# Where the third block's output projection stands, and which buffers wait for which

## The chip, the cores and the metric

The kernel runs on one core of one Trainium2 chip. The core has a matrix engine (TensorE, PE in the profile), VectorE (DVE), ScalarE (ACT), GpSimd (POOL) and SyncE (SP), which in this kernel issues all the data transfers in one queue. The metric is the device time of one execution in microseconds. Three runs of the kernel before took 2527.12, 2529.54 and 2530.48 us; the median is 2529.54 us.

## The reference

One decoder layer on 2112 tokens, 2048 of a prompt and 64 of eight running sequences, in f32. An input projection feeds two mixers, whose 512 + 512 rows are concatenated; an output projection, a norm and a SwiGLU feed-forward layer follow.

```
y5, h_re, h_im = s5_mixer(u, ...)          # ends in a GLU
yh, S_hg = hgrn2_mixer(q, fz, iv, og, ...) # 4 heads of 128
x = x + concatenate([y5, yh]) @ w_out      # 1024 x 1024
h2 = rmsnorm(x, norm_ffn)
x = x + (silu(h2 @ w_gate) * (h2 @ w_up)) @ w_down   # 2816 wide
y = rmsnorm(x, norm_final)
```

## The kernel before

Activations are stored feature by feature: 128 features on the partitions, tokens along the row. The mixers work through four groups of tokens and four heads, 16 heads in all. Beside the last heads, the generator `sides` (line 1332) runs the S5 mixer and its GLU, which writes its rows into the DRAM tensor `y_s`; each HGRN2 head writes its 128 rows there too.

What follows runs over three blocks of `FT = 704` tokens and has three kinds of product: the output projection (`mix`, matmul outputs named `o`), gate and up (`g`, `u`) and down (`d`). Each is done by a 2 x 2 block scheme with seven products in place of eight (`seven`, line 1073). Seven combinations of the activations, called slots here, meet seven combinations of the weights. Four of the seven slots are differences of the four quarters, made by `combine` (line 975). Every operand is split into a high and a low part (`xh`, `xl` for the activations, `wh`, `wl` for the weights), and a product is three matmuls of 128 x 352. One slot with two weight matrices is 24 matmuls.

- `combine_y` (line 988) makes the slots of block b for the projection: for each of four feature tiles it loads two row blocks of `y_s` (tile `cy`), makes four differences into `ct`, and stores them in DRAM as `ty_s`. For block 0 it runs in a pool `cmb` of two buffers, so that one tile follows the other; for blocks 1 and 2 it runs in the staging pool `xraw` (tiles `xr`).
- `x_slots` (line 1006) loads a slot into a staging tile `xr`, and ACT and DVE split it into `xh` and `xl`, for which there are 7 buffers, later 8. The staging pool has 1 buffer until block 0's projection is under way and 2 afterwards.
- `w_prep` (line 1020) loads two weight matrices at a time, makes their combinations in block 0 only, and splits them into `wh` and `wl`.
- `mix` adds the products on accumulators `acc`, eight tiles of 128 x 704 loaded from `xT`, and stores them in `x1_s`. `norm2` (line 1203) sums the squares (`sum_f`), brings the sum over the partitions with two pairs of small matmuls (`ss_f`, then `pr_f`), scales the eight accumulators in place (line 1207), makes the difference slots `ht` and stores all seven in `h_s`.
- `ffn` (line 1227) loads the slots of `h_s`, runs gate and up over 11 column pairs in three chunks `CH` of 4, 4 and 3, whose results become slots in `s_s`, and then down. The tiles `s`, `u` and `T` of gate and up come from the pool `hp2`.

The order before is: heads, `combine_y(0)`, `mix(0)`, `combine_y(1)` and `combine_y(2)`, `mix(1)` with `norm2(0)` after its first seven steps, `mix(2)` with `norm2(1)` likewise, `norm2(2)`, then `ffn` for the three blocks, each with the final norm of the block before inside it. A pool that is opened where another was closed takes over its memory, and its tiles wait for the last users of that memory (`reuse_waits`). `acc2` (4 accumulators) and the `ht` pool `mt` are closed before `hp2` is opened. A scheduling layer then orders the instructions on each engine; on the chip each engine works through its own list in order.

Of the kernel before, what the change touches and what calls it, by code (L numbers as in the profile page):

```python
# [9 lines left out]
F32 = mybir.dt.float32  # L10
# [8 lines left out]
P = 128  # L19
# [906 lines left out]
def glu(e, pool, ps, w):  # L926
    nc = e.nc
    wh, wl = w
    NB_ = 44
    W = NB_ * L  # L930
    for n0 in range(0, NCK, NB_):
        g = pool.tile([P, 4, L, NB_], F32, tag="gg", name=f"gg{n0}")
        for k in range(4):
            nc.sync.dma_start(g[:, k], e.g_s[k * P:(k + 1) * P, :, n0:n0 + NB_])
        hi = pool.tile([P, 4, L, NB_], F32R, tag="ghi", name=f"ghi{n0}")
        lo = pool.tile([P, 4, L, NB_], F32R, tag="glo", name=f"glo{n0}")
        nc.scalar.activation(hi, g, AF.Copy)
# [62 lines left out]
def y_slots(e, b):  # L1000
# [201 lines left out]
def norm2(e, b, x):  # L1202
    nc = e.nc
    r = norm_r(e, x, f"f{b}")
    for j in range(4):
        for d in (j, j + 4):
            nc.vector.scalar_tensor_tensor(x[d], x[d], e.gain[:, KD + d:KD + d + 1], r, op0=ALU.mult, op1=ALU.mult)
        B = [x[d][:, h * FH:h * FH + FH] for d in (j, j + 4) for h in range(2)]
        T = e.mtmp.tile([P, 4, FH], F32, tag="mt", name=f"ht{b}_{j}")
        combine(nc.vector, [T[:, i] for i in range(4)], *B)  # L1210
        dst = e.h_s[b]
        for slot, t in ((0, B[0]), (1, B[2]), (4, B[3])):
            nc.sync.dma_start(dst[:, slot, j], t)
        nc.sync.dma_start(dst[:, 2:4, j], T[:, 0:2])
        nc.sync.dma_start(dst[:, 5:7, j], T[:, 2:4])
# [8 lines left out]
            nc.sync.dma_start(e.o["yT"][d * P:(d + 1) * P, b * FT:(b + 1) * FT], x[d])  # L1224


def ffn(e, b, got):
    X = x_slots(e, [e.h_s[b][:, i] for i in range(7)], 4, f"h{b}")
    for c, (f0, nk) in enumerate(CH):
        for j in range(nk):  # L1230
            f = (f0 + j, f0 + nk + j)
            s = {}
            nm = f"{f[0]}_{b}"
            W = w_prep(e, [([e.i[w][i] for i in f], f"{n}{f[0]}") for w, n in (("w_gate_u", "g"), ("w_up_u", "u"))], 4, b)
            mats = [(W[0], gate_sink(e, s, nm), "g" + nm), (W[1], up_sink(e, s, nm, e.s_s[b][c], j), "u" + nm)]
            for _ in seven(e, mats, X, 4):
                yield
    x = acc_tiles(e, b, e.x1_s, f"d{b}")
    got["x"] = x
    for c, (f0, nk) in enumerate(CH):  # L1240
        X = x_slots(e, [e.s_s[b][c][:, i, :nk] for i in range(7)], nk, f"s{b}_{c}")
        cs = slice(f0 * P, (f0 + 2 * nk) * P)
        for g in range(2):
            js = (2 * g, 2 * g + 1)
            W = w_prep(e, [([e.i["w_down_u"][d][:, cs] for d in (j, j + 4)], f"wd{j}_{c}") for j in js], nk, b)
            mats = [(w, acc_sink(e, x[j], x[j + 4]), f"d{j}_{b}_{c}") for w, j in zip(W, js)]
            for _ in seven(e, mats, X, nk):
                yield


def run(gen, n=None):
    r = None
    i = 0
    while n is None or i < n:
        try:
            r = next(gen)
        except StopIteration:
            return r, True
        i += 1
    return r, False  # L1260
# [3 lines left out]
def body(ctx, tc, ins, outs, scratch=None, stop=9):  # L1264
    e = Env()
# [149 lines left out]
    for b in range(FB):
        ff = ffn(e, b, got[b])
        run(ff, 14)
        if b:
            final(e, b - 1, got[b - 1]["x"])
        run(ff)  # L1420
# [58 lines left out]
```

## Time and profile before

| what | value |
|---|---|
| median of three runs | 2529.54 us |
| profiled execution, its span | 2525.47 us, 2523.7 us |
| PE busy | 2313.9 us, 92% |
| DVE, ACT, POOL busy | 67%, 40%, 16% |
| mean granted TensorE clock | 0.958 |

The program has three parts. Until 829 us the mixers run, with PE busy throughout; from there to some 1174 us the projections and the first norms, with PE often idle; then gate, up and down until 2500 us. The last 24 us are the final norm of the last block. Busy shares of the whole say little here, since the middle part has limits of its own.

### The profile page before, as it was taken

The numbers are of one execution on the slowest core, as the hardware profiler recorded it, in microseconds if no ns is written. First come the engines' busy times: TensorE is split into PE (matmuls) and PEld (weight loads), VectorE is DVE, ScalarE is ACT, GpSimd is POOL, SyncE is SP. The second block draws the span as 40 slices with busy tenths as digits, with TensorE's granted clock in tenths as the row PEclk, the third lists the DMA queues.
The fourth block names the chain that finished last, engine by engine and source line by source line (L and its number), as shares of the span: only waits on it lengthen the run. The fifth ranks groups of instructions, "written<-read, shape, count | busy, mean of one in ns | idle before, by whom it ended". The sixth has DMA issues, their size and how long they took to land.

```text
span 2523.7 us, 44154 instructions
## 1 busy us (share of the span) xinstructions
PE 2313.9 (92%) x16933; PEld 2162.1 (86%) x16933; DVE 1700.1 (67%) x3222; ACT 1013.0 (40%) x1860; POOL 416.4 (16%) x807
## 2 busy tenths in 40 slices
PE   6999999999998463975999999999999999999997
PEld 5888777777787463965999999999999999999996
DVE  7936354555556575986777799865557786565776
ACT  4332323232222231642444544644455454444452
POOL 5209593948211000000000000000000000000000
PEclk9999999999999786987999999999999999999998
DMA  9696556444545679875665566676457567644752
GB/s 268 178 273 222 159 189 182 141 137 135 171 144 167 218 270 311 313 283 199 225 221 207 224 253 240 221 278 225 173 197 267 200 225 261 242 177 166 274 209 90
DMA packets 269317, 538.53 MB, mean 213 GB/s; under 512 B 82089, under 2 KB 172530, under 8 KB 256050
## 3 DMA queue, kind: packets, MB, share of 16 engines
q1 hardware_dynamic: 269106, 535.71, 61.9%
q8 instruction: 133, 2.18, 0.3%
q14 instruction: 78, 0.64, 0.1%
HBM read 373.06 MB, written 162.56 MB: 212 GB/s over the span
## 4 chain that ended last, share of the span: by engine, by line
PE 70%; DMA 10%; DVE 9%; POOL 7%; issue 2%; ACT 2%; SPq 1%; DVEq 0%; ACTq 0%; POOLq 0%
PE pA_u L1091 10%; PE pA_g L1091 10%; PE pA_d L1091 8%; PE pB_u L1091 5%; PE pB_g L1091 5%; PE pB_d L1091 4%; PE ps_v L263 3%; PE ps_u L263 3%; PE pQ_g L1091 3%; PE pQ_u L1091 2%; PE pQ_d L1091 2%; PE ps_f L263 2%; PE pz L263 2%; DMA cy<-y_s 2%; PE ps_q L263 2%
## 5 line engine op out<-in xcount | busy, mean ns | idle before, releaser
L1047 DVE TENSOR_TENSOR wl_g<-wr_g,wh_g 128x512 fp32r<-128x512 f32 x231 | 158.6, 687 | 114.2 <-ACT wh_g L1046 112.6
L290 POOL TENSOR_TENSOR r_z<-st_z,mhalf 128x2 f32<-128x2 f32 (+1 forms) x12 | 9.0, 765 | 1355.4 <-DVE st_z L289 1355.4
L1047 DVE TENSOR_TENSOR wl_u<-wr_u,wh_u 128x512 fp32r<-128x512 f32 x231 | 158.7, 688 | 98.5 <-ACT wh_u L1046 97.6
L1046 ACT ACTIVATE wh_g<-wr_g 128x512 fp32r<-128x512 f32 x231 | 144.6, 628 | 167.6 <-PE pA_g L1091 70.2
L1046 ACT ACTIVATE wh_wd<-wr_wd 128x512 fp32r<-128x512 f32 (+1 forms) x252 | 140.3, 589 | 176.1 <-DMA wr_wd<-in_w_down_u 81.2
L1046 ACT ACTIVATE wh_u<-wr_u 128x512 fp32r<-128x512 f32 x231 | 144.3, 628 | 151.3 <-DMA wr_u<-in_w_up_u 39.5
L1091 PE MATMUL pA_g<-xh_h,wh_g 128*128 128x352 f32 x528 | 172.9, 328 | 30.7 <-ACT s L1118 22.9
L1091 PE MATMUL pA_g<-xh_h,wl_g 128*128 128x352 f32 x528 | 172.6, 327 | 6.0 <-DVE wl_g L1047 6.0
L1091 PE MATMUL pA_g<-xl_h,wh_g 128*128 128x352 f32 x528 | 171.3, 324 | 0.0
L1091 PE MATMUL pA_d<-xh_s,wh_wd 128*128 128x352 f32 x528 | 170.3, 323 | 0.4 <-DVE acc_d L1106 0.4
L1091 PE MATMUL pA_u<-xh_h,wh_u 128*128 128x352 f32 x528 | 170.5, 323 | 0.0
L1091 PE MATMUL pA_u<-xh_h,wl_u 128*128 128x352 f32 x528 | 170.4, 323 | 0.0
L1091 PE MATMUL pA_d<-xl_s,wh_wd 128*128 128x352 f32 x528 | 169.5, 321 | 0.0
L1091 PE MATMUL pA_u<-xl_h,wh_u 128*128 128x352 f32 x528 | 169.5, 321 | 0.0
L1091 PE MATMUL pA_d<-xh_s,wl_wd 128*128 128x352 f32 x528 | 169.1, 322 | 0.0
L1047 DVE TENSOR_TENSOR wl_wd<-wr_wd,wh_wd 128x512 fp32r<-128x512 f32 (+1 forms) x252 | 156.9, 641 | 16.5 <-ACT wh_wd L1046 16.4
L1091 PE MATMUL pA_o<-xh_y,wh_wo 128*128 128x352 f32 x192 | 65.2, 348 | 73.4 <-ACT xh_y L1014 47.2
L1091 PEld LDWEIGHTS pA_g<-xh_h,wh_g 128*128 128x128 f32 x528 | 100.4, 190 | 31.8 <-ACT s L1118 23.4
L504 DVE TENSOR_TENSOR q<-q,tot 128x256 f32<-128x256 f32 (+1 forms) x96 | 53.0, 552 | 95.2 <-PE p L477 34.5
L1091 PEld LDWEIGHTS pA_g<-xh_h,wl_g 128*128 128x128 f32 x528 | 100.7, 191 | 6.3 <-DVE wl_g L1047 6.3
L1091 PEld LDWEIGHTS pA_o<-xh_y,wh_wo 128*128 128x128 f32 x192 | 38.4, 203 | 76.7 <-ACT xh_y L1014 48.4
L1015 DVE TENSOR_TENSOR xl_s<-xr_s,xh_s 128x1408 fp32r<-128x1408 f32 (+1 forms) x63 | 94.4, 1499 | 11.1 <-ACT xh_s L1014 10.6
(503 smaller groups left out, 7314.7 us busy)
## 6 DMA issues: line engine op xcount, KB each, us to landing
xr_s<-s_s SPq DMA_DIRECT2D x42, 704.0 KB, 5.8
s_s<-T SPq DMA_DIRECT2D x132, 176.0 KB, 1.9
wr_g<-in_w_gate_u SPq DMA_DIRECT2D x44, 512.0 KB, 3.5
wr_u<-in_w_up_u SPq DMA_DIRECT2D x44, 512.0 KB, 6.9
wr_g<-sum_g SPq DMA_DIRECT2D x22, 1024.0 KB, 5.8
wr_u<-sum_u SPq DMA_DIRECT2D x22, 1024.0 KB, 9.2
s_s<-s SPq DMA_DIRECT2D x99, 176.0 KB, 2.3
wr_wd<-in_w_down_u SPq DMA_DIRECT2D x32, 512.0 KB, 5.9
```

Of the source, the lines that this page charges most:

```text
L263: e.nc.tensor.matmul(out, whl[k][a], xhl[k][b], start=start and i == 0, stop=stop and i == len(seq) - 1)
L290: nc.gpsimd.tensor_tensor(r[:rows, a:b], st[:rows, a:b], e.mhalf[:rows, 0:b - a], op=ALU.pow)
L504: vec.tensor_tensor(qv[:, :, 1], qv[:, :, 1], t[:, :, 0:1].to_broadcast(shp), op=ALU.mult)
L1015: nc.vector.tensor_tensor(lo, raw, hi.bitcast(F32), op=ALU.subtract)
L1046: nc.scalar.activation(hi, src, AF.Copy)
L1047: v.tensor_tensor(lo, src, hi.bitcast(F32), op=ALU.subtract)
L1091: nc.tensor.matmul(ps, W[i][w][:, ks], X[i][x][:, k], start=first and k == 0 and c == 0, stop=i in (1, 4, 6) and k == nk - 1 and c == 2, s ...
```

## The change

- `combine_y` yields after every second feature tile, and `sides` now runs it for blocks 0 and 1 in the pool `cmb`. The GLU yields once per 352 tokens and not twice.
- `ffn` is split into `gate_up`, which takes a list of chunks, and `down`. Block 0 runs gate and up for chunks 0 and 1 with `norm2(1)` and `combine_y(2)` inside, then `mix(2)`, then chunk 2 with `norm2(2)` inside, then down. The slots of block 0 are loaded a second time for chunk 2.
- The slots keep 7 buffers throughout. The staging pool has 2 from the start.
- `acc2`, `nrm` and `hp2` are opened together, so that they no longer share memory, and 12 accumulators stay in use to the end. The tiles `ht` come from the staging pool.

```
-            combine_y(e, 0, cp)
+            for b in (0, 1):
+                for _ in combine_y(e, b, cp):
+                    yield
...
-    px, pw, pr, pq = pool("xs", 7), pool("ws", 7), pool("wr", 2), pool("xr", 1)
+    px, pw, pr, pq, pa = pool("xs", 7), pool("ws", 7), pool("wr", 2), pool("xr", 2), pool("acc", 8)
...
-    px2, pw2, pq2 = pool("xs2", 1), pool("ws2", 3), pool("xr2", 1)
-    e.xs.set((px, 7), (px2, 1))
+    pw2 = pool("ws2", 3)
...
+    e.nrm, pa2, e.hp = pool("nrm", 2), pool("acc2", 4), pool("hp2", 6)
...
-        for b in (1, 2):
-            combine_y(e, b, Cmb(e))
-        e.acc.set((pa2, 4), (pa, 8))
-        for b in (1, 2):
-            mg = mix(e, b, got[b])
-            run(mg, 7)
-            norm2(e, b - 1, got[b - 1]["x"])
-            run(mg)
-        norm2(e, 2, got[2]["x"])
-    e.hp = pool("hp2", 6)
-    e.acc.set((pa, 8))
+    e.acc.set((pa2, 4), (pa, 8))
+    mg = mix(e, 1, got[1])
+    run(mg, 7)
+    norm2(e, 0, got[0]["x"])
+    run(mg)
+    cy = combine_y(e, 2, Cmb(e))
+    for i, _ in enumerate(gate_up(e, 0, (0, 1))):
+        if i == 0:
+            norm2(e, 1, got[1]["x"])
+        if i in (3, 5):
+            run(cy, 1)
+    run(mix(e, 2, got[2]))
+    for i, _ in enumerate(gate_up(e, 0, (2,))):
+        if i == 0:
+            norm2(e, 2, got[2]["x"])
+    run(down(e, 0, got[0]))
```

On SP, behind the last heads, the kernel before loads and stores the four tiles of block 0 (`cy0`, `ct0`) and then goes on to the slots of `mix(0)` (`xr_y0`):

```order
L997 DMA ty_s0_67<-ct0_2_8860 512x1x352
L995 DMA cy0_3_8868<-y_s_62 128x704 x2
L997 DMA ty_s0_67<-ct0_3_8869 512x1x352
L1011 DMA xr_y0_1_9251<-y_s_62 128x4x352
L1011 DMA xr_y0_2_9257<-ty_s0_67 128x1408
```

At the same place on SP the changed kernel has the four tiles of block 1 (`cy1`, `ct1`) in between:

```order
L996 DMA ty_s0_67<-ct0_3_8609 512x1x352
L994 DMA cy1_0_8682<-y_s_62 128x704 x2
L996 DMA ty_s1_68<-ct1_0_8683 512x1x352
L994 DMA cy1_1_8691<-y_s_62 128x704 x2
L996 DMA ty_s1_68<-ct1_1_8692 512x1x352
L994 DMA cy1_2_8741<-y_s_62 128x704 x2
L996 DMA ty_s1_68<-ct1_2_8742 512x1x352
L994 DMA cy1_3_8750<-y_s_62 128x704 x2
L996 DMA ty_s1_68<-ct1_3_8751 512x1x352
L1012 DMA xr_y0_2_9290<-ty_s0_67 128x1408
```

The sums of blocks 0 and 1 stand next to each other now, and those of block 0 stand where they stood.

On PE, the kernel before has the norm of block 0 between the last matmul of `mix(0)` (`pA_o3_0`) and the first of `mix(1)` (`pA_o0_1`):

```order
L1091 MATMUL pA_o3_0_9857<-xh_y0_6_9283,wl_wo3_0_6_9840 128x352
L1191 MATMUL ss_f0_0_10532<-ones_100,sum_f0_10508 128x1 x2
L1191 MATMUL ss_f0_0_10532<-ones_100,sum_f0_10508 96x1
L1197 MATMUL pr_f0_0_10545<-dg_f0_0_10542,ones_100 128x128 x2
L1197 MATMUL pr_f0_0_10545<-dg_f0_0_10542,ones_100 128x96
L1191 MATMUL ss_f0_1_10550<-ones_100,sum_f0_10508 128x1 x2
L1191 MATMUL ss_f0_1_10550<-ones_100,sum_f0_10508 96x1
L1197 MATMUL pr_f0_1_10563<-dg_f0_1_10560,ones_100 128x128 x2
L1197 MATMUL pr_f0_1_10563<-dg_f0_1_10560,ones_100 128x96
L1091 MATMUL pA_o0_1_10320<-xh_y1_0_10216,wh_wo0_1_0_10260 128x352
```

In the changed kernel the norm of block 0 stands inside `mix(1)` on PE; 222 rows lie between the last matmul of `mix(0)` and the second `pr_f0`. It is the norm of block 1 that stands at a border, between `mix(1)` (`pA_o3_1`) and the first gate and up column (`pA_g0_0`, `pA_u0_0`):

```order
L1092 MATMUL pA_o3_1_10652<-xh_y1_6_10210,wl_wo3_1_6_10635 128x352
L1192 MATMUL ss_f1_0_11190<-ones_100,sum_f1_11166 128x1 x2
L1192 MATMUL ss_f1_0_11190<-ones_100,sum_f1_11166 96x1
L1092 MATMUL pA_g0_0_10950<-xh_h00_0_10836,wh_g0_0_0_10880 128x352
L1092 MATMUL pA_u0_0_10965<-xh_h00_0_10836,wh_u0_0_0_10888 128x352
L1198 MATMUL pr_f1_0_11203<-dg_f1_0_11200,ones_100 128x128 x2
L1092 MATMUL pA_g0_0_10950<-xl_h00_0_10837,wh_g0_0_0_10880 128x352
```

Between the first and the second of the two norm products two gate matmuls stand now, and nothing else.

On DVE, the first addition of the second half of `mix(1)` (`acc2_m1`) stands in the kernel before among weight splits, well behind `norm2(0)`:

```order
L1047 TENSOR_TENSOR wl_wo3_1_0_10629<-wr_wo3_1_10624,wh_wo3_1_0_10628 128x512
L1047 TENSOR_TENSOR wl_wo2_1_1_10633<-wr_wo2_1_10616,wh_wo2_1_1_10632 128x512
L1106 TENSOR_TENSOR acc1_m1_10202<-acc1_m1_10202,pB_o1_1_10390 128x352
L1047 TENSOR_TENSOR wl_wo3_1_1_10637<-wr_wo3_1_10624,wh_wo3_1_1_10636 128x512
L1047 TENSOR_TENSOR wl_wo2_1_2_10641<-wr_wo2_1_10616,wh_wo2_1_2_10640 128x512
L1106 TENSOR_TENSOR acc2_m1_10206<-acc2_m1_10206,pA_o2_1_10680 128x352
```

In the changed kernel it stands directly behind `norm2(0)`: eight scalings, then 16 instructions on `ht` and on the first gate and up weights, of which these are the last, then the addition:

```order
L1048 TENSOR_TENSOR wl_u0_0_0_10889<-wr_u0_0_10884,wh_u0_0_0_10888 128x512
L1054 TENSOR_TENSOR wr_u0_0_10884<-wr_u0_0_10884 128x512
L982 TENSOR_TENSOR ht0_0_10528<-acc4_m0_9264,ht0_0_10528 128x352
L1055 TENSOR_TENSOR wr_g0_0_10876<-wr_g0_0_10876 128x512
L1062 TENSOR_TENSOR wr_g0_0_10876<-wr_g0_0_10876 128x512
L982 TENSOR_TENSOR ht0_1_10540<-acc5_m0_9268,ht0_1_10540 128x352
L1055 TENSOR_TENSOR wr_u0_0_10884<-wr_u0_0_10884 128x512
L1062 TENSOR_TENSOR wr_u0_0_10884<-wr_u0_0_10884 128x512
L984 TENSOR_TENSOR ht0_0_10528<-acc4_m0_9264,ht0_0_10528 128x352
L1061 TENSOR_TENSOR wr_g0_0_10876<-wr_g0_0_10876 128x512
L1107 TENSOR_TENSOR acc2_m1_10164<-acc2_m1_10164,pA_o2_1_10638 128x352
```

The weight work of the first gate column has moved ahead of that addition, and `norm2(0)` next to it.

## Rows read from the trace of the kernel before

**Rows 1.** Stretches: us, then busy us (count) of PE, PEld, DVE, ACT, POOL, clock, DMA.

```profile
829.00:848.50 19.50, 0.51 (x3) 0.11 (x1) 6.14 (x11) 0.67 (x2) 0.00 (x0) 0.50 0.82 284
848.50:926.00 77.50, 64.34 (x336) 59.86 (x336) 54.56 (x87) 30.47 (x44) 0.00 (x0) 0.91 0.58 207
926.00:987.10 61.10, 5.80 (x24) 5.21 (x24) 33.27 (x65) 7.08 (x11) 2.43 (x4) 0.52 0.88 303
987.10:1086.60 99.50, 97.94 (x600) 96.78 (x600) 83.40 (x123) 56.51 (x76) 3.04 (x4) 0.97 0.77 281
1086.60:1173.70 87.10, 43.64 (x215) 41.65 (x216) 65.31 (x108) 20.40 (x29) 2.81 (x4) 0.69 0.83 296
1173.70:1200.00 26.30, 24.92 (x155) 24.64 (x155) 18.41 (x34) 12.42 (x25) 0.00 (x0) 1.00 0.38 132
1200.00:2480.00 1280.00, 1278.92 (x7994) 1277.80 (x7993) 936.63 (x1605) 632.01 (x1093) 6.58 (x8) 1.00 0.61 223
```

**Rows 2.** Timeline of PE: start, us, instruction, idle before it and what ended that.

```profile
848.51 0.66 PE L1091 MATMUL pA_o<-xh_y,wh_wo 128*128 128x352 f32 x1 [19.00 <-ACT wh_wo L1046]
987.13 0.66 PE L1091 MATMUL pA_o<-xh_y,wh_wo 128*128 128x352 f32 x1 [45.41 <-ACT xh_y L1014]
1170.58 0.66 PE L1091 MATMUL pA_g<-xh_h,wh_g 128*128 128x352 f32 x1 [22.45 <-ACT s L1118]
```

**Rows 3.** Timeline of ACT, just before the first and the last of these.

```profile
847.83 1.15 ACT L1046 ACTIVATE wh_wo<-wr_wo 128x512 fp32r<-128x512 f32 x2 [20.50 <-DMA ty_s<-ct]
...
1170.07 0.46 ACT L1118 ACTIVATE s<-pA_g 128x352 f32<-128x352 f32 x1 [21.43 <-DVE ht L984]
```

**Rows 4.** Timeline of the SP queue: loads and stores of the sums.

```profile
809.30 0.90 SPq L995 DMA_DIRECT2D cy<-y_s  x2
...
826.72 0.55 SPq L997 DMA_DIRECT2D ty_s<-ct  x1
...
835.33 0.53 SPq L997 DMA_DIRECT2D ty_s<-ct  x1
...
843.60 0.53 SPq L997 DMA_DIRECT2D ty_s<-ct  x1
...
977.41 0.53 SPq L997 DMA_DIRECT2D ty_s<-ct  x1
```

**Rows 5.** Timeline of PE: end of block 0's projection and its norm.

```profile
925.62 0.32 PE L1091 MATMUL pA_o<-xh_y,wl_wo 128*128 128x352 f32 x1
930.72 1.33 PE L1191 MATMUL ss_f<-ones,sum_f 128*128 128x1 f32 x6 [4.77 <-DVE sum_f L1184]
935.12 1.57 PE L1197 MATMUL pr_f<-dg_f,ones 128*128 128x128 f32 x6 [3.07 <-DVE dg_f L297]
...
940.16 1.57 PE L1197 MATMUL pr_f<-dg_f,ones 128*128 128x128 f32 x6 [1.58 <-DVE dg_f L297]
```

**Rows 6.** Timeline of DVE behind that norm: the eight scalings.

```profile
942.26 6.99 DVE L1207 SCALAR_TENSOR_TENSOR acc_m<-acc_m,gain,rr_f 128x704 f32<-128x704 f32 x8 [1.87 <-ACT rr_f L1198]
```

**Rows 7.** Timeline of the SP queue: load of a second-half accumulator of `mix(1)`.

```profile
951.02 0.33 SPq L1154 DMA_DIRECT2D acc_m<-in_xT  x1
```

**Rows 8.** Lines of DVE, 1000 to 1500 us: count, busy us, mean ns, idle before.

```profile
L1047 DVE TENSOR_TENSOR wl_g<-wr_g,wh_g 128x512 fp32r<-128x512 f32 x77 | 53.0, 688 | 35.1 <-ACT wh_g L1046 35.0
...
L1015 DVE TENSOR_TENSOR xl_s<-xr_s,xh_s 128x1408 fp32r<-128x1408 f32 x11 | 17.8, 1620 | 1.9 <-ACT xh_s L1014 1.9
...
L982 DVE TENSOR_TENSOR ht<-acc_m 128x352 f32<-128x352 f32 x8 | 4.2, 522 | 13.2 <-DMA h_s<-ht 13.1
```

**Rows 9.** Lines of ACT, 1200 to 2480 us: the high part of a slot.

```profile
L1014 ACT ACTIVATE xh_s<-xr_s 128x1408 fp32r<-128x1408 f32 x42 | 57.6, 1374 | 24.3 <-DMA xr_s<-s_s 24.3
```

**Rows 10.** The page's DMA issues: count, KB each, median us to landing.

```profile
xr_s<-s_s SPq DMA_DIRECT2D x42, 704.0 KB, 5.8
```

More of the change, by code (lines that the diff above doesn't have):

```diff
@@ L953, in glu @@
                     nc.sync.dma_start(e.y_s[rows, o:o + (a1 - a0) * L], fl[:, (a0 - n0) * L:(a1 - n0) * L])
-            if f % 2:
-                yield
+        yield
 FT = 704
@@ L997, in combine_y @@
         nc.sync.dma_start(e.ty_s[b][:, :, j], T)
+        if j % 2:
+            yield
 def y_slots(e, b):
@@ L1208, in norm2 @@
         B = [x[d][:, h * FH:h * FH + FH] for d in (j, j + 4) for h in range(2)]
-        T = e.mtmp.tile([P, 4, FH], F32, tag="mt", name=f"ht{b}_{j}")
+        T = e.xraw.tile([P, 4, FH], F32, tag="xr", name=f"ht{b}_{j}")
         combine(nc.vector, [T[:, i] for i in range(4)], *B)
@@ L1224, in final, with gate_up @@
             nc.sync.dma_start(e.o["yT"][d * P:(d + 1) * P, b * FT:(b + 1) * FT], x[d])
-def ffn(e, b, got):
-    X = x_slots(e, [e.h_s[b][:, i] for i in range(7)], 4, f"h{b}")
-    for c, (f0, nk) in enumerate(CH):
+def gate_up(e, b, chunks):
+    X = x_slots(e, [e.h_s[b][:, i] for i in range(7)], 4, f"h{b}{chunks[0]}")
+    for c in chunks:
+        f0, nk = CH[c]
         for j in range(nk):
@@ L1236, in ffn, with down @@
             for _ in seven(e, mats, X, 4):
-                yield
+                pass
+            yield
+def down(e, b, got):
     x = acc_tiles(e, b, e.x1_s, f"d{b}")
@@ L1247, in ffn @@
             for _ in seven(e, mats, X, nk):
-                yield
+                pass
+            yield
 def run(gen, n=None):
@@ L1342, in sides @@
         with tc.tile_pool(name="cmb", bufs=2, reuse_waits="tile") as cp:
-            combine_y(e, 0, cp)
-        yield
+            for b in (0, 1):
+                for _ in combine_y(e, b, cp):
+                    yield
     side = sides()
@@ L1377, in body @@
     e.tags = {e.ps_mm: "mm", e.ps_x: "x"}
-    px, pw, pr, pq = pool("xs", 7), pool("ws", 7), pool("wr", 2), pool("xr", 1)
-    e.nrm, pa = pool("nrm", 2), pool("acc", 8)
-    e.xs, e.ws, e.wraw, e.xraw, e.acc = Rot((px, 7)), Rot((pw, 7)), Rot((pr, 2)), Rot((pq, 1)), Rot((pa, 8))
+    px, pw, pr, pq, pa = pool("xs", 7), pool("ws", 7), pool("wr", 2), pool("xr", 2), pool("acc", 8)
+    e.xs, e.ws, e.wraw, e.xraw, e.acc = Rot((px, 7)), Rot((pw, 7)), Rot((pr, 2)), Rot((pq, 2)), Rot((pa, 8))
     e.psA, e.psQ = Rot((e.ps_mm, 2)), Rot((e.ps_x, 2))
@@ L1390, in body @@
     rt.close()
-    px2, pw2, pq2 = pool("xs2", 1), pool("ws2", 3), pool("xr2", 1)
-    e.xs.set((px, 7), (px2, 1))
+    pw2 = pool("ws2", 3)
     e.ws.set((pw, 7), (pw2, 3))
-    e.xraw.set((pq, 1), (pq2, 1))
     pA2, pQ2 = pool("psA2", 1, space=PSUM), pool("psQ2", 2, space=PSUM)
@@ L1397, in body @@
     e.tags[pA2], e.tags[pQ2] = "a2", "q2"
-    with ExitStack() as cm:
-        pa2 = cm.enter_context(tc.tile_pool(name="acc2", bufs=4, reuse_waits="tile"))
-        e.mtmp = cm.enter_context(tc.tile_pool(name="mt", bufs=1, reuse_waits="tile"))
-        run(mg)
-        e.psA.set((e.ps_mm, 2), (pA2, 1))
-        e.psQ.set((e.ps_x, 2), (pQ2, 2))
-        for b in (1, 2):
-            combine_y(e, b, Cmb(e))
-        e.acc.set((pa2, 4), (pa, 8))
-        for b in (1, 2):
-            mg = mix(e, b, got[b])
-            run(mg, 7)
-            norm2(e, b - 1, got[b - 1]["x"])
-            run(mg)
-        norm2(e, 2, got[2]["x"])
-    e.hp = pool("hp2", 6)
-    e.acc.set((pa, 8))
[L1415 to L1420, printed above, removed]
+    e.nrm, pa2, e.hp = pool("nrm", 2), pool("acc2", 4), pool("hp2", 6)
+    run(mg)
+    e.psA.set((e.ps_mm, 2), (pA2, 1))
+    e.psQ.set((e.ps_x, 2), (pQ2, 2))
+    e.acc.set((pa2, 4), (pa, 8))
+    mg = mix(e, 1, got[1])
+    run(mg, 7)
+    norm2(e, 0, got[0]["x"])
+    run(mg)
+    cy = combine_y(e, 2, Cmb(e))
[9 more added lines that the diff above has]
+    run(down(e, 0, got[0]))
+    for b in range(1, FB):
+        for i, _ in enumerate(gate_up(e, b, (0, 1, 2))):
+            if i == 1:
+                final(e, b - 1, got[b - 1]["x"])
+        run(down(e, b, got[b]))
     final(e, FB - 1, got[FB - 1]["x"])
```

## The prediction

> **What bounds the kernel now.** I read PE's busy time by stretches first, since PE does nearly all the work and the question is where it stands still. From 1200 us on it issues 7994 matmuls in 1280 us without a gap [rows 1], which gives 0.160 us for one and says that nothing else can be saved there. The same price turns every earlier stretch into work and loss:
>
> - 848.5 to 926 (`mix(0)`): 336 matmuls are 53.8 us of 77.5, so 23.7 are lost.
> - 926 to 987.1: no projection at all, 61.1 lost.
> - 987.1 to 1086.6: 576 matmuls are 92.2 us of 99.5; 7.3 lost.
> - 1086.6 to 1173.7: 215 less 24 small ones of the norm are 191, or 30.6 us of 87.1; 56.5 lost.
>
> Together 149 us, and 19 more before 848.5. Next come PE's own waits: three long ones of 19.00, 45.41 and 22.45 us [rows 2]. ACT's rows say what stood behind the first and last [rows 3]: the first weight split waited for a store of `ct`, because its buffer lies on memory of `cmb`; the gate tile `s` waited for the last `ht` difference, because `hp2` lies on memory of `mt`. The SP queue shows behind the second one the eight tiles of blocks 1 and 2, the last of which is stored at 977.41 [rows 4]. The smaller losses of `mix(0)` come from one staging buffer: load, ACT and DVE follow each other for every slot.
>
> **Term 1, the start of `mix(0)`: 33 us more.** The change puts the four tiles of block 1 in `cmb` too. The order shows them on SP behind block 0's, and block 0's first load behind the GLU's last store, as before. On DVE their differences stand ahead of `xl` of the first slot, and the first weight split still waits for `cmb`'s last store, which is block 1's now. So the sums do not form beside the heads; the wait at 829 gets longer. The last two undisturbed rounds took 835.33 - 826.72 = 8.61 and 843.60 - 835.33 = 8.27 us [rows 4]. Nothing else runs then, so I take 4 x 8.27 = 33.1 (bounds 31, for rounds somewhat quicker, and 36).
>
> **Term 2, `mix(0)` with two staging buffers: 18 us less.** The nearest rows are `mix(1)` and `mix(2)`, which have two buffers and lose 7.3 us in 576 matmuls, the restart at the lower clock included [rows 1]. For 336 that is 4.3 by share and 7.3 if all of it is the restart; I take 5.5 in place of 23.7. Above: nothing gained, since block 0 also makes the weight sums.
>
> **Term 3, between `mix(0)` and `mix(1)`: 45 us less.** The load and store rounds of blocks 1 and 2 are gone from here. The norm of block 0 takes 940.16 - 925.62 = 14.5 us from the last matmul to its second `pr_f` [rows 5]; the order puts 222 rows of PE, some 35 us, into that time, which hide it. A new wait follows. The second half of `mix(1)` accumulates on buffers that `norm2(0)` frees, and its first addition stands on DVE behind it. From the second `pr_f` it is 2.1 us to the scalings, 7.0 for the eight [rows 5, 6], then 9 instructions of 128 x 512 at 0.688 and 7 of 128 x 352 at 0.522 [rows 8], 9.9 us: 19.0 in all. PE has 24 matmuls meanwhile, 3.8 us. It waits 15.2, and with one more for the clock 16 of 61.1 remain. Below: 951.02 - 940.16 = 10.9 to the issue of the accumulator's load [rows 5, 7], less 3.8, or 7. Above: 26, if the load is late by its flight and DVE by some splits. Behind the waiting addition stand the weight splits of the first gate column, which are wanted only later.
>
> **Term 4, the start of gate and up: 40 us less.** `hp2`, `acc2` and the tiles `ht` no longer share memory, so the wait of 22.45 goes, and `norm2(2)` and half of `mix(2)` leave this place. What is late next is `norm2(1)`. It stands on PE at the border with two gate matmuls between `ss_f` and `pr_f`. In the rows of block 0 PE waits 4.77 before `ss_f`, and `pr_f` starts 4.40 after it [rows 5]: 9.2 us. DVE comes next. By the order it has, to the end of the second column, 46 instructions of 128 x 512, 42 of 128 x 352, 10 of 128 x 704 and 7 of 128 x 1408, that is 31.6 + 21.9 + 8.7 + 11.3 = 73.5 us by the means [rows 6, 8], against 336 matmuls, 53.8 us, of PE. Back to back they overlap, parts of the norm run during the 9.2, and the last of these results are not PE's to wait for; I charge 5 (bounds 0 and 20) and 2 for the clock: 16 in place of 56.5. Bounds 9 and 31.
>
> **Term 5, gate and up with guests: 2 us more.** The seven slots loaded again cost 7 x 1.37 us of ACT and 7 x 1.62 of DVE [rows 8, 9], `norm2(2)` 15 instructions of 128 x 704 and 16 of 128 x 352, some 22 us of DVE by the same means, `combine_y(2)` 16 more, 8 us. They are hidden by gate and up, where DVE is busy 937 of 1280 us [rows 1]; without that cover they would cost 40. `mix(2)` itself is the same work at another place. The loads of `cy2` and of accumulators wait in the SP queue ahead of weight loads, but ten weight buffers are five slots, 19 us of PE. Bounds 0 and 15 (1 us at each change of slots).
>
> **Sum.** 33.1 - 18.2 - 45.1 - 40.5 + 2 = -68.7 us. The profiled execution took 2525.5 (1.8 outside its span), which gives 2456.8. It lies 4 below the median of the runs, so I predict 2460.
>
> **Rivals.**
>
> *The sums do run beside the heads.* Then PE starts near 829 and neither the 33 nor the 19 us are paid: 2460 - 52 = 2408. For it speaks the place where they are written, against it SP's order and `cmb`'s memory, free only after the GLU.
>
> *Half of it is eaten.* Weight sums and norms make DVE the bound in `mix(0)` and the first two gate columns: term 2 gains nothing (18 more), term 4 takes all of the 20 (15 more): 2493. For it: in the stretch to 1173.7 DVE had 65.3 busy us for 30.6 of matmuls. Against it: from 987.1 to 1086.6 it had 83.4 of 99.5 and PE hardly stopped [rows 1].
>
> *Seven buffers for seven slots: slower.* A new set can be split only as the old one is used up. If PE had to wait at each change for one slot's whole path, 5.8 for the load, 1.37 on ACT and 1.62 on DVE [rows 8 to 10], it would lose 8.8 us at each of 15 changes, 132 in all: 2592. From 69 / 15 = 4.6 us a change on, nothing is gained. Against it: the first buffer comes free six slots, 6 x 24 x 0.160 = 23 us, before the old set ends, and the changes with eight buffers after 1200 show no idle time at all. The Trainium skill, in Perfetto Trace Analysis, section Optimization Strategy, reads a gap that repeats on the engine that should be full as a sign of too few buffers for the next tile. By that rule the gap would repeat here at every change; no row before shows one.
>
> **How the numbers follow.** The forecast has 0.72, early sums 0.06, the eaten half 0.15, seven buffers 0.07. Terms at their good ends (31 more, losses of 4.3, 8 and 10, nothing for term 5) sum to -88 and give 2441, and the range reaches down to 2430 for part of the first rival; at the other side several bounds together and the second rival give 2500. Range 2430 to 2500. What a measurement can tell from no change is 0.2%, 5 us. Faster by more than that is 0.92, within 0.02, slower 0.06, nearly all of it the third rival.
>
> **What would show it.** In the trace after: PE's first `pA_o` near 882, ended by ACT, which waited for a `ty_s` store; eight loads and stores of `cy` and `ct` in a row from 809; `mix(0)` done some 59 us later; a wait of about 15 us inside `mix(1)` on an addition on `acc_m`; some 10 us at the border to gate and up; from there a full PE at 0.160 us a matmul, with `mix(2)` inside. Wrong would be: a start before 860, several microseconds of idle time at each change of slots, or a wait of over 20 us that none of this names.

## The result and the profile after

The changed kernel takes 2467.64 us (median of four runs, 2464.68 to 2470.30), 0.9756 of the time before, 95% interval 0.9739 to 0.9773. The forecast was 2460 in a range of 2430 to 2500. The profiled execution took 2465.9 us, its span is 2464.1. PE is busy 2296.9 us, 93% of it. The heads end at 829.3 us, as they did before (829.5), so the whole gain lies behind them.

The stretches of the changed kernel, cut at the places of the forecast's terms; the columns are those of [rows 1]:

```profile
829.25:878.59 49.34, 0.01 (x2) 0.00 (x1) 15.38 (x28) 0.68 (x2) 0.00 (x0) 0.50 0.67 226
878.59:937.00 58.41, 56.76 (x339) 56.19 (x340) 53.27 (x80) 33.60 (x47) 0.00 (x0) 0.96 0.73 266
937.00:977.65 40.65, 40.65 (x263) 40.36 (x261) 36.38 (x61) 23.35 (x36) 3.54 (x4) 1.00 0.67 244
977.65:1014.30 36.65, 19.11 (x103) 18.48 (x103) 31.92 (x61) 9.90 (x14) 1.22 (x2) 0.79 1.01 366
1014.30:1375.00 360.70, 358.64 (x2226) 356.88 (x2226) 312.74 (x543) 180.60 (x319) 10.53 (x6) 0.99 0.77 281
1375.00:1394.97 19.97, 5.36 (x18) 4.87 (x18) 12.39 (x20) 6.66 (x9) 0.00 (x0) 0.57 0.97 369
1394.97:2420.00 1025.03, 1021.30 (x6377) 1018.38 (x6376) 739.86 (x1250) 508.55 (x860) 6.27 (x8) 1.00 0.61 223
```

Read the PE column against the length. The first row is nothing but waiting, `mix(0)` is nearly full where it lost 23.7 us before, and from 1394.97 on PE stops for 4 us in 1025. Two stretches stand out: 977.65 to 1014.30, which the forecast names, and 1375 to 1394.97, which it does not. PE's own waits at these places, in answer to [rows 2]:

```profile
878.59 0.66 PE L1092 MATMUL pA_o<-xh_y,wh_wo 128*128 128x352 f32 x1 [49.34 <-ACT wh_wo L1047]
990.24 0.66 PE L1092 MATMUL pA_o<-xh_y,wh_wo 128*128 128x352 f32 x1 [12.59 <-DVE acc_m L1107]
1011.99 0.78 PE L1192 MATMUL ss_f<-ones,sum_f 128*128 128x1 f32 x6 [3.12 <-DVE sum_f L1185]
1014.26 0.66 PE L1092 MATMUL pA_g<-xh_h,wh_g 128*128 128x352 f32 x1 [1.49 <-ACT xh_h L1015]
1388.94 0.95 PE L1092 MATMUL pA_d<-xh_s,wh_wd 128*128 128x352 f32 x2 [13.91 <-ACT xh_s L1015]
```

The long wait at the start of `mix(0)` is ended by the same weight split as in [rows 3], and ACT waited for the same kind of store:

```profile
877.91 1.15 ACT L1047 ACTIVATE wh_wo<-wr_wo 128x512 fp32r<-128x512 f32 x2 [49.70 <-DMA ty_s<-ct]
```

On the SP queue, eight stores of sums stand in a row where [rows 4] had four. Three of them; undisturbed rounds take 7.7 us:

```profile
843.00 0.53 SPq L996 DMA_DIRECT2D ty_s<-ct  x1
...
866.06 0.52 SPq L996 DMA_DIRECT2D ty_s<-ct  x1
...
873.73 0.53 SPq L996 DMA_DIRECT2D ty_s<-ct  x1
```

On DVE, the eight scalings of `norm2(0)` and, behind them and 16 other instructions, the addition that the second wait is for. DVE has no idle time between the two rows:

```profile
974.29 6.99 DVE L1208 SCALAR_TENSOR_TENSOR acc_m<-acc_m,gain,rr_f 128x704 f32<-128x704 f32 x8
...
989.67 0.52 DVE L1107 TENSOR_TENSOR acc_m<-acc_m,pA_o 128x352 f32<-128x352 f32 x1
```

The last wait is new. In front of the start of `down(0)` DVE is full, 33.80 of 35 us, as this stretch shows:

```profile
1340.00:1375.00 35.00, 34.15 (x211) 33.61 (x209) 33.80 (x65) 12.87 (x26) 0.00 (x0) 1.00 0.85 305
```

and in the SP queue the last stores of `ht` (line 1216) come just ahead of the first loads of `down(0)`'s slots (line 1012):

```profile
1370.08 0.37 SPq L1216 DMA_DIRECT2D h_s<-ht  x1
...
1373.29 0.36 SPq L1216 DMA_DIRECT2D h_s<-ht  x1
...
1380.16 1.14 SPq L1012 DMA_DIRECT2D xr_s<-s_s  x2
...
1390.58 2.05 SPq L1012 DMA_DIRECT2D xr_s<-s_s  x2
```

The list of what SP waited for from 1376 to 1393 us (total, times, longest) names, among others, a store of `ht` for line 1012:

```profile
SPq L1012 <- DMA h_s<-ht: 0.5, 1, 0.5
```

The store at 1373.29 landed at 1380.15, and the load was issued at 1380.16. DVE had finished the last `ht` difference at 1369.2; its store went out 4 us later, behind other transfers of the queue, and took 6.9 us to land. The load, which stands behind it in the queue, then waited only 0.5 us for the buffer itself and landed at 1387.49.

### The profile page after: what moved, and what is told of

Its sections match the earlier page's. It is cut to its first block, busy times and chain, and to the rows that moved or that the text cites. A ratio compares the mean times of both kernels' runs of the same rounds, so it can differ in the third digit from the quotient of the medians.

```text
span 2464.1 us, 44177 instructions
## 1 busy us (share of the span) xinstructions
PE 2296.9 (93%) x16933; PEld 2148.7 (87%) x16933; DVE 1703.9 (69%) x3229; ACT 1017.7 (41%) x1867; POOL 424.5 (17%) x807
## 4 chain that ended last, share of the span: by engine, by line
PE 72%; DVE 8%; DMA 8%; POOL 7%; issue 2%; SPq 1%; ACT 1%; DVEq 0%; ACTq 0%; POOLq 0%
PE pA_u L1092 10%; PE pA_g L1092 9%; PE pA_d L1092 8%; PE pB_u L1092 5%; PE pB_g L1092 5%; PE pB_d L1092 4%; PE ps_v L263 3%; PE ps_u L263 3%; PE pA_o L1092 3%; PE pQ_g L1092 2%; PE pQ_u L1092 2%; PE pQ_d L1092 2%; PE ps_f L263 2%; PE pz L263 2%; PE ps_g L263 2%; PE ps_q L263 2%
## 5 line engine op out<-in xcount | busy, mean ns | idle before, releaser
L1092 PE MATMUL pA_o<-xh_y,wh_wo 128*128 128x352 f32 x192 | 63.7, 332 | 62.3 <-ACT wh_wo L1047 49.3
L1092 PEld LDWEIGHTS pA_d<-xh_s,wh_wd 128*128 128x128 f32 x528 | 99.8, 189 | 16.0 <-ACT xh_s L1015 14.2
L1015 ACT ACTIVATE xh_s<-xr_s 128x1408 fp32r<-128x1408 f32 (+1 forms) x63 | 80.4, 1277 | 58.6 <-DMA xr_s<-s_s 49.8
```

The source lines that it names most:

```text
L1092: nc.tensor.matmul(ps, W[i][w][:, ks], X[i][x][:, k], start=first and k == 0 and c == 0, stop=i in (1, 4, 6) and k == nk - 1 and c == 2, s ...
```

## The experiments

All are edits of the changed kernel. Up to the last matmul of the heads each of them shows the same 7465 PE instructions, at most ten of them at another place in the order, and yet this point came between 828.80 and 838.65 us in the 14 profiled executions. So the profiles are compared by the rest, the span less that point. The times have their own intervals.

| run | time, us | of before (95%) | heads' end | rest |
|---|---|---|---|---|
| before | 2529.61 | 1 | 829.5 | 1694.2 |
| after | 2467.64 | 0.9756 (0.9739 to 0.9773) | 829.3 | 1634.8 |
| s1_one_block | 2449.95 | 0.9697 (0.9673 to 0.9720) | 833.7 | 1616.2 |
| cmb_four | 2450.51 | 0.9700 (0.9680 to 0.9720) | 831.6 | 1613.8 |
| one_staging | 2492.32 | 0.9860 (0.9834 to 0.9885) | 833.8 | 1658.5 |
| acc_eight | 2480.77 | 0.9811 (0.9789 to 0.9833) | 838.7 | 1640.5 |
| mix2_front | 2532.00 | 1.0017 (1.0003 to 1.0031) | 828.8 | 1698.1 |
| ht_own | 2465.87 | 0.9756 (0.9733 to 0.9779) | 834.8 | 1628.6 |
| mix2_sooner | 2478.35 | 0.9813 (0.9784 to 0.9842) | 830.2 | 1641.2 |
| mix2_six | 2453.53 | 0.9706 (0.9683 to 0.9730) | 832.0 | 1617.8 |
| all_three | 2429.76 | 0.9615 (0.9592 to 0.9639) | 829.9 | 1595.6 |
| two_of_three | 2431.18 | 0.9619 (0.9604 to 0.9635) | 832.1 | 1594.5 |
| half_block | 2425.84 | 0.9595 (0.9578 to 0.9611) | 835.6 | 1589.2 |
| acc_on_cmb | 2442.16 | 0.9653 (0.9629 to 0.9678) | 837.8 | 1605.9 |

**The sums ahead of `mix(0)` (term 1): s1_one_block and cmb_four.**

```
-            for b in (0, 1):
-                for _ in combine_y(e, b, cp):
-                    yield
+            for _ in combine_y(e, 0, cp):
+                yield
...
-    run(mg)
+    cy = combine_y(e, 1, Cmb(e))
+    while not run(mg, 3)[1]:
+        run(cy, 1)
+    run(cy)
```

> Only block 0's sums stay in the pool of two buffers; block 1's are made in the staging pool inside mix(0). Theory (term 1: the four rounds of block 1 are paid in full ahead of mix(0)): the first projection matmul comes near 848.5 in place of 878.59, mix(0) takes at most 5 us longer, since DVE has 53.3 busy us of 58.4 there and gets 16 more subtractions of 0.52 us; the time is near 2440 (2435 to 2447). Rival (the work only changes place: DVE and the transfers of mix(0) have no room): the start moves, but mix(0) and the start of mix(1) take back 20 us or more, the time stays above 2458.

PE's start and the norm of block 0 in this kernel:

```profile
853.09 0.66 PE L1092 MATMUL pA_o<-xh_y,wh_wo 128*128 128x352 f32 x1 [19.40 <-ACT wh_wo L1047]
...
916.82 1.33 PE L1192 MATMUL ss_f<-ones,sum_f 128*128 128x1 f32 x6 [4.90 <-DVE sum_f L1185]
922.37 1.56 PE L1198 MATMUL pr_f<-dg_f,ones 128*128 128x128 f32 x6 [4.22 <-DVE dg_f L297]
```

The wait is back at 19.40, 29.9 us less: four rounds were paid in full. `mix(0)` takes 58.8 us in place of 58.1, so it had room for the sums. But of the 29.9 us only 18.6 reach the end: with `mix(1)`'s slots later, the order puts block 0's norm at a border again. The theory holds for the start; the time missed its bounds by 3 us.

```
-        with tc.tile_pool(name="cmb", bufs=2, reuse_waits="tile") as cp:
+        with tc.tile_pool(name="cmb", bufs=4, reuse_waits="tile") as cp:
```

> All eight sums stay ahead of mix(0), but their pool has four buffers in place of two, so that in the SP queue the next load stands ahead of the store. Theory (a round is a chain of load, subtractions and store, 8.27 us, in which the transfers are busy 0.57 of the time): a round falls to some 4.7 us, and the first projection matmul comes 20 to 25 us sooner, near 855; time near 2444. Rival (the transfers themselves set the round): the rounds stay at 8 us, start near 878, time 2467.

The stores of sums in the SP queue with four buffers:

```profile
839.67 0.52 SPq L996 DMA_DIRECT2D ty_s<-ct  x1
847.09 0.53 SPq L996 DMA_DIRECT2D ty_s<-ct  x1
850.76 0.53 SPq L996 DMA_DIRECT2D ty_s<-ct  x1
854.76 4.44 SPq L996 DMA_DIRECT2D ty_s<-ct  x2
```

Undisturbed rounds fall to 3.7 to 4.0 us from 7.7, so two buffers made each round a chain of load, subtractions and store. The first rounds, with the loads of accumulators among them, still take 6 to 8, and the wait ends at 32.00 and not at some 25. With 17.3 us less at the start and 21.0 in the rest the theory holds, its size was too large.

**One staging buffer in `mix(0)` (term 2): one_staging.**

```
-    px, pw, pr, pq, pa = pool("xs", 7), pool("ws", 7), pool("wr", 2), pool("xr", 2), pool("acc", 8)
+    px, pw, pr, pq, pa = pool("xs", 7), pool("ws", 7), pool("wr", 2), pool("xr", 1), pool("acc", 8)
...
-    pw2 = pool("ws2", 3)
+    pw2, pq2 = pool("ws2", 3), pool("xr2", 1)
+    e.xraw.set((pq, 1), (pq2, 1))
```

> One staging buffer until mix(0) is under way, as before; all else as in the changed kernel. Theory (term 2: with one buffer the load, ACT and DVE follow each other for every slot): mix(0) takes some 76 us in place of 58, the time rises by 18 to 2486 (2479 to 2490). Rival (mix(0) lost its time for other reasons, such as the sums or memory that it had to wait for): under 8 us more, 2475 or less.

The stretch of `mix(0)` in this kernel:

```profile
886.09:961.50 75.41, 64.66 (x337) 60.53 (x337) 56.00 (x79) 36.59 (x49) 0.00 (x0) 0.89 0.60 213
```

75.4 us in place of 58.1, as the theory says; the time, 2492.3, lies 2 us above its bounds. The rest is 23.7 longer; besides the 17.3 of this stretch, the wait at the start grows by 2.9 and the one at `down(0)` by 2.0.

**The wait inside `mix(1)` (term 3): acc_eight.**

```
-    pw2 = pool("ws2", 3)
+    pw2 = pool("ws2", 2)
...
-    e.nrm, pa2, e.hp = pool("nrm", 2), pool("acc2", 4), pool("hp2", 6)
+    e.nrm, pa2, e.hp = pool("nrm", 2), pool("acc2", 8), pool("hp2", 4)
...
-    e.acc.set((pa2, 4), (pa, 8))
+    e.acc.set((pa2, 8), (pa, 8))
```

> The changed kernel with 8 + 8 accumulators, so that none of mix(1)'s second half takes a buffer of mix(0) (room from one weight buffer of ten and from hp2 with 4 in place of 6). The first addition of that half no longer depends on norm2(0), but stands on DVE behind its scalings still. Theory (term 3: DVE's order is the wait): at least 9 of the 12.59 us at 990.24 stay. Rival (the late load of the accumulator, landed at 988.91, is the wait): under 4 us stay there. The time itself may go either way by some us, since the gate tiles have fewer buffers: 2455 to 2480.

PE's waits from there to the gate, and on DVE an addition of the second half ahead of the scalings:

```profile
996.08 0.40 PE L1092 MATMUL pB_o<-xh_y,wh_wo 128*128 128x352 f32 x1 [1.35 <-DVE acc_m L1107]
...
1020.54 1.30 PE L1192 MATMUL ss_f<-ones,sum_f 128*128 128x1 f32 x6 [10.63 <-DVE sum_f L1185]
```

```profile
987.04 0.52 DVE L1107 TENSOR_TENSOR acc_m<-acc_m,pQ_o 128x352 f32<-128x352 f32 x1 [0.45 <-PE pQ_o L1092]
987.48 6.98 DVE L1208 SCALAR_TENSOR_TENSOR acc_m<-acc_m,gain,rr_f 128x704 f32<-128x704 f32 x8
```

The wait of 12.59 is gone, which is the rival's number, but the kernel does not answer the question. The expectation said that the addition still stood behind the scalings; freed of the shared accumulators, it moved ahead of them. What is shown is that the wait hangs on accumulators shared with `norm2(0)`. What was the last of it is told by the changed kernel's own trace: the load landed at 988.91, but DVE worked without a gap until the addition began at 989.67. So DVE's order came last there, by 0.8 us, and without it the load would have left nearly the whole wait. The loss came back as 10.63 us at the next norm, since its sum of squares got late.

**Where `mix(2)` stands (terms 4 and 5): mix2_front, ht_own, mix2_sooner, mix2_six.**

```
...
+    run(combine_y(e, 2, Cmb(e)))
+    mg = mix(e, 2, got[2])
+    run(mg, 7)
+    norm2(e, 1, got[1]["x"])
+    run(mg)
+    norm2(e, 2, got[2]["x"])
+    run(gate_up(e, 0, (0, 1, 2)))
```

> The changed kernel with mix(2) back in front of gate and up: combine_y(2), mix(2) with norm2(1), then norm2(2), as before; the buffers stay apart. Theory (term 4: 22.45 us of the 40 came from pools apart, the rest from norms that no longer stand at a border): no wait of 20 us on the gate tile s, but two norms of 12 to 15 us at borders, on PE, each with a restart at the lower clock (5 to 8), while the 14 us at down(0) and the clock there (8) go: 10 to 25 us more than the changed kernel, 2478 to 2493. Rival (pools apart did all of it): 2467 or less.

PE's waits at the start of `mix(2)` and of gate and up:

```profile
1052.41 0.96 PE L1092 MATMUL pA_o<-xh_y,wh_wo 128*128 128x352 f32 x2 [24.88 <-ACT xh_y L1015]
...
1160.19 0.66 PE L1092 MATMUL pA_g<-xh_h,wh_g 128*128 128x352 f32 x1 [31.52 <-ACT xh_h L1015]
```

ACT's rows there name the loads of slots:

```profile
1050.99 1.38 ACT L1015 ACTIVATE xh_y<-xr_y 128x1408 fp32r<-128x1408 f32 x1 [22.95 <-DMA xr_y<-y_s]
...
1158.76 1.38 ACT L1015 ACTIVATE xh_h<-xr_h 128x1408 fp32r<-128x1408 f32 x1 [29.59 <-DMA xr_h<-h_s]
```

Both expectations were far too low: 2532.0, no gain at all on before. The gate tile `s` is no longer waited for, so pools apart do what they say; but 31.52 us of waiting for slots, behind `norm2(2)`, stand in the place of the 22.45 of [rows 2]. The SP queue shows why these slots are late: their first load goes out when a store of `ht` has landed, at 1152.57.

```profile
1148.13 0.41 SPq L1216 DMA_DIRECT2D h_s<-ht  x1
...
1152.58 3.58 SPq L1012 DMA_DIRECT2D xr_h<-h_s  x2
```

The kernel before, whose `ht` had memory of its own, issued the first of these loads 100 us sooner, and 84 gate and up matmuls ran between 1090 and 1141, inside `mix(2)` and the norms:

```profile
1051.80 0.32 SPq L1011 DMA_DIRECT2D xr_h<-h_s  x1
```

So mix2_front puts back the place of `mix(2)`, but keeps `ht` in the staging pool. It shows that in the changed kernel pools apart gain nothing without the move. It does not show what they would gain with `mix(2)` in front and `ht` in a buffer of its own; no run has that.

```
-        T = e.xraw.tile([P, 4, FH], F32, tag="xr", name=f"ht{b}_{j}")
+        T = e.htp.tile([P, 4, FH], F32, tag="ht", name=f"ht{b}_{j}")
...
-    pw2 = pool("ws2", 3)
+    pw2 = pool("ws2", 2)
...
+    e.htp = pool("htp", 1)
```

> The tiles ht of norm2 get one buffer of their own instead of the staging pool (room for it comes from one of the ten weight buffers). Theory (down(0) starts late since its slots wait for the staging buffers that norm2(2)'s ht tiles hold until their stores have landed at 1380): the wait of 13.91 us at 1388.94 shrinks to under 5 and the 7 us or so of lower clock around it go; time near 2450 (2446 to 2456). Rival (DVE and the SP queue are late there whatever the buffers, DVE busy 33.8 of 35 us before it): the wait stays above 9 us, time 2463 or more.

Two stretches of this kernel, the start of gate and up and the start of `down(0)`, and the first slot loads of `down(0)` in the SP queue:

```profile
1024.00:1046.00 22.00, 12.79 (x50) 11.77 (x51) 13.31 (x23) 6.01 (x8) 2.44 (x4) 0.53 0.86 310
1375.00:1400.00 25.00, 24.22 (x150) 23.93 (x150) 25.00 (x42) 12.94 (x21) 0.00 (x0) 1.00 1.03 397
```

```profile
1315.84 2.66 SPq L1012 DMA_DIRECT2D xr_s<-s_s  x2
```

At `down(0)` the theory on the buffers is right: the first loads go out at 1315.84 and not at 1380.16, and PE has no wait there above 2 us and the full clock, though DVE is busy 25.00 of 25 us. The time is not: both norm products of `norm2(1)` now stand together behind `mix(1)`, with most of the first gate column behind them (48 of its 168 matmuls have moved into `mix(1)`), and that stretch runs at a granted clock of 0.53. PE's loss from 1375 us on to the middle of `down(0)` falls by some 13 us, and that at the start of gate and up grows by some 12.

```
-    for i, _ in enumerate(gate_up(e, 0, (0, 1))):
+    for i, _ in enumerate(gate_up(e, 0, (0,))):
...
-        if i in (3, 5):
+        if i in (1, 2):
...
-    for i, _ in enumerate(gate_up(e, 0, (2,))):
+    for i, _ in enumerate(gate_up(e, 0, (1, 2))):
```

> mix(2) moves from behind chunk 1 to behind chunk 0 of gate and up, so that norm2(2) stands four columns ahead of the start of down(0). Both theories on the hole at down(0) (staging buffers held by ht, or DVE late with norm2(2)) expect the wait of 13.91 us to go, 14 to 21 us less, time 2447 to 2455. Against both: if the load of new slots of block 0's first intermediate or of the accumulators is what is late, the wait at the start of down(0) stays above 9 us, time 2463 or more. A new wait may come up where mix(2) now begins, if block 2's sums are not ready.

```profile
1153.59 0.66 PE L1092 MATMUL pA_o<-xh_y,wh_wo 128*128 128x352 f32 x1 [26.26 <-ACT xh_y L1015]
```

That row of PE is the start of `mix(2)`: the wait at `down(0)` is gone, and a longer one is here. The SP queue just before it:

```profile
1145.98 0.52 SPq L996 DMA_DIRECT2D ty_s<-ct  x1
1146.61 3.98 SPq L1012 DMA_DIRECT2D xr_y<-y_s  x2
```

The first slot's load, for which PE waits, went out right behind the last store of `ct` and landed at 1152.13. The second was issued at 1150.21, when that store had landed at 1150.20. It is the same pair of staging buffers, held by the sums of block 2.

`mix2_six` cuts gate and up by columns, 6 and 5, with the sums behind columns 2 and 4.

> mix(2) stands behind the sixth column of gate and up in place of the eighth, so that norm2(2) is five columns ahead of down(0); the sums of block 2 are made behind columns 2 and 4. Theory (the hole at down(0) is the staging buffers held by norm2(2)'s ht tiles until their stores land; with two more columns, 96 matmuls of 0.160 us each, they are free in time): no wait above 2 us at the start of down(0), none above 5 at the start of mix(2), the lower clock there goes too; 20 us less than the changed kernel, time near 2447 (2442 to 2453). Rival (the wait at mix(2) that came with the fourth column, 26.26 us, is paid in another size here, since its slots need the same two staging buffers): 8 us or more at the start of mix(2), time 2455 or more.

The start of `mix(2)` on PE, and the stretch around the start of `down(0)`:

```profile
1192.46 0.43 PE L1092 MATMUL pA_o<-xh_y,wh_wo 128*128 128x352 f32 x1 [1.51 <-ACT xh_y L1015]
```

```profile
1360.00:1400.00 40.00, 40.00 (x252) 40.00 (x251) 39.72 (x62) 23.14 (x35) 0.00 (x0) 1.00 0.80 296
```

PE is full at `down(0)` and waits 1.51 us at `mix(2)`. The rest is 17.0 us shorter, the whole of what this place had cost. The PE order up to the first gate columns is that of the changed kernel, so nothing else moved. Against the median the gain is 14, just outside the theory's bounds. (A column is 168 matmuls, not the 96 of the expectation, so the two columns are 54 us of PE.)

**The edits together: all_three, two_of_three, half_block, acc_on_cmb.** The first is s1_one_block, cmb_four and mix2_six in one; the second leaves block 1's sums where the changed kernel has them.

> Block 1's sums inside mix(0), four buffers for block 0's, and mix(2) behind the sixth column. If the three places add up: start of mix(0) 34 us sooner than in the changed kernel (15 us behind the heads in place of 49), down(0) without its hole (20 us), less some 11 us that block 0's norm costs when its sums stand in front of mix(1): 2424 (2408 to 2430). If one eats another (the transfers and DVE in mix(0) with its slots arriving sooner): 2435 or more.

> Four buffers for the sums of both blocks ahead of mix(0), and mix(2) behind the sixth column; block 1's sums are not moved. If the two edits add up: by the places, 21 us from the start of mix(0) and 17 from down(0) on the changed kernel, 2429 (2424 to 2436), the same as with all three, since what block 1's sums cost at the start the exposed norm cost there. If moving block 1's sums was worth its 15 us of earlier start: 2440 or more.

Both come out at the same time. all_three starts `mix(0)` 17.2 us sooner behind the heads (14.93 for 32.15). Of this 12.3 us are lost again by the end of `mix(1)`, where block 0's norm stands at a border, and the others behind it; what costs those was not separated. The third puts two of block 1's four tiles on each side:

> As all_three, but two of block 1's four tiles of sums stand in the pool of four ahead of mix(0) and only two in mix(0). Theory (the norm of block 0 came to stand at a border because mix(1)'s slots came late; with half the sums ready, the order has PE rows of mix(1) around it again): start of mix(0) about 7 us later than in all_three, near 852, but no 12 us at the norm with the lower clock around it; 2420 (2412 to 2426). Rival (the wait moves to mix(1)'s first additions behind norm2(0) on DVE, 12 us): 2428 or more, no better than all_three.

```profile
860.27 0.66 PE L1094 MATMUL pA_o<-xh_y,wh_wo 128*128 128x352 f32 x1 [24.71 <-ACT wh_wo L1049]
...
986.17 0.66 PE L1094 MATMUL pA_o<-xh_y,wh_wo 128*128 128x352 f32 x1 [5.16 <-DVE acc_m L1109]
...
994.02 0.66 PE L1094 MATMUL pA_g<-xh_h,wh_g 128*128 128x352 f32 x1 [4.01 <-ACT xh_h L1017]
```

These rows of PE are all its waits over 2 us from the heads to the end of block 0's down product. The norm no longer stands at a border, and 5.16 us remain of the wait inside `mix(1)`. The start came 10 us later behind the heads than in all_three, not 7, and the time is just inside the theory's bounds. At 0.9595 it is the fastest run here and beats both kernels; its interval overlaps that of all_three.

> As half_block, but the accumulators' pool is opened ahead of the weight buffers' pool, so that the accumulators and not the weight buffers lie on the memory of cmb. What is asked: is it memory or the sums themselves that holds the start of mix(0)? Theory (memory holds only the first two slots, which need no sums): the first weight split no longer waits for a store of ct and comes near 832 in place of 859; PE can start on 48 matmuls (7.7 us) of slots 0 and 1, then waits for slot 2, which the sums hold; and the accumulators' loads, eight of some 0.9 us in the SP queue, now stand ahead of slot 2: mix(0) ends 0 to 5 us sooner behind the heads' end, time 2420 to 2428. Rival (memory is the whole wait): mix(0) ends 15 us sooner or more, time below 2415.

```profile
856.16 0.66 PE L1094 MATMUL pA_o<-xl_y,wh_wo 128*128 128x352 f32 x1 [17.19 <-DVE xl_y L1018]
...
872.19 0.66 PE L1094 MATMUL pB_o<-xh_y,wh_wo 128*128 128x352 f32 x1 [6.04 <-ACT xh_y L1017]
```

The weight split came at 815.54, so it had been held by memory alone. But the kernel is 16 us slower than half_block, and both expectations are wrong on the time. The accumulators' loads, now behind the sums' memory, went out from 858.26 to 861.52, and the first slot that needs sums behind them at 862.37, 24.6 us behind the heads' end, where half_block has it at 21.6. `mix(0)` ended 85.7 us behind the heads and not 82.3. The other 13 us were lost later, and no run was made for them.

## Why the prediction was right, and where it was not

Losses of PE by stretch (length less matmuls of the blocks at 0.160 us, as in [rows 1]), what the terms left of them and what the trace after shows:

| place | before | forecast | after |
|---|---|---|---|
| start of `mix(0)` | 19.0 | 52.1 | 49.3 |
| `mix(0)` | 23.7 | 5.5 | 4.4 |
| to the end of `mix(1)`; `mix(2)` | 61.1 + 7.3 | 16 + 7.3 | 18.3 |
| gate and up with guests | 56.5 | 16 + 2 | 16.7 |
| start of `down(0)` | 0 | 0 | 17.3 |

- **Term 1** was right in mechanism and nearly in size: 30.3 us for 33.1, as a round took 7.7 us and not 8.27. s1_one_block shows that block 1's rounds are the whole of it.
- **Term 2** was right: 19.3 for 18.2, and one_staging gives 17.3 of it back.
- **Term 3** was right in its place, 12.59 us for 15.2. The 16 instructions behind the scalings took 8.5 us (981.20 to 989.67) and not the 9.9 that their means add up to. The norm of block 0 was hidden. acc_eight shows that the shared accumulators are the cause; that DVE's order came last, with the load 0.8 us ahead of it, is read from the one trace.
- **Term 4** named the two gaps of the border, but 3.12 and 1.49 us remain where it charged 9.2 and 5. Its account of the gain is not settled. In mix2_front the pools are apart, and the wait of 22.45 is only replaced by one of 31.52, so pools apart alone earn nothing there and the move of `mix(2)` and `norm2(2)` is needed. But that wait comes from `ht` in the staging pool, which is a part of the change too; how the 40 us divide between the move and the memory is not shown.
- **Term 5** is the step that failed: 2 us with bounds 0 and 15, measured 17.3 at the start of `down(0)`. It hid `norm2(2)` in the average load of DVE, 937 of 1280 us. In the 35 us in question DVE was busy 33.80, its `ht` differences came late, and their tiles occupy the two staging buffers through which `down(0)`'s slots must come. ht_own and mix2_six each remove the wait, one by buffers and one by time. Of the 3.4 us beside the wait of 13.91 the clock makes up some 2: behind the wait the matmuls start 0.29 us apart until 1394.9, the 1.2 GHz level, and 0.16 apart, the 2.4 GHz level, from there on. The granted clock from 1375 to 1394.97 is 0.57.
- **Seven buffers** lost nothing: behind 1394.97 PE stops for 4 us in 1025, over all changes of slots there. The rule beside that rival, from the Trainium skill, Perfetto Trace Analysis, section Optimization Strategy (the same gap repeating on the engine that should be full can mean too few buffers), does not show at those seven. The traces agree with it for the staging pool: with one buffer there, one_staging has five gaps of 1.07 to 2.49 us for slots inside `mix(0)`, and with two the changed kernel has none as long. The gaps of 13.91, 26.26, 24.88 and 31.52 us are of another kind, since each stands alone; all end with a slot load that came out behind `ct` or `ht` tiles in the two staging buffers, and one buffer more, for `ht`, ended the first.
- The sum came out 9 us low: 17.3 us at `down(0)` that no term held, and some 2 more behind it, against 1 to 5 too much at each of the other places, 10 together. That the total is so near is in part luck.

## What to carry to other kernels

Work that is put "beside" a full engine should be priced against the busy share of the engine that does it in that very stretch, not over the whole; and one should follow what its tiles hold until their stores land. When a temporary moves into a pool that feeds the next stage, the next stage's first load is what to look at. Where a wait is removed by giving buffers apart, look who stands in line behind it: in mix2_front the wait for `hp2`'s memory went, and a longer one for the staging buffers took its place.

## What the runs showed of the hardware

- The same 7465 PE instructions, in nearly the same order, took from 828.80 to 838.65 us in 14 profiled executions, one of each kernel. The changed kernel (829.25) and acc_eight (838.65) have the instructions of every engine and of the SP queue in the same order up to there, so spans of single profiles can differ by nearly 10 us ahead of the first edited instruction. Whether the place of the tiles in memory has a part in it is not shown.
- DVE instructions of 128 x 352, shown with 0.52 us each, start 0.43 us apart when back to back (981.20, 981.64, 982.07 in the changed kernel), and those of 128 x 512, shown with 0.69, 0.60 apart. Sums of mean durations overstate such a queue by some 15%: 9.9 us for the 16 instructions of term 3, which took 8.5.
- With four buffers in place of two, a round of load, four subtractions and store fell from 7.7 us to between 3.7 and 4.0.
